# A hybrid decoder layer on one core: all tiles that TensorE reads at equal addresses modulo 256 bytes, V and index weights in three loads

## The chip, the cores and the metric

The kernel runs on one core of one Trainium2 chip. The metric is the device time of one execution in microseconds; several executions are timed, and their median is given.

## The reference

One decoder layer for 512 tokens of width 1,024, in float32. The input is normalised and multiplied by one wide matrix, whose columns feed two branches: a recurrent one (a short causal convolution, two gates, a scan over the tokens) and an attention one with 8 heads, in which index queries and keys choose 256 keys for each token. The branches are gated and added, then come an output projection, a gated channel mixer of width 3,072 with a convolution of length 3, and a gated embedding of the layer.

```
xn = _rmsnorm(x, mix_norm[l])
h = xn @ w_in[l]
lru_x, lru_gate, q, k, v, qi, ki, wi, gate_a, gate_b = _split_cols(h)
ya = (_rg_lru(...) * jax.nn.gelu(lru_gate)) @ w_lru_br[l]
yb = _dsa_attention(qh, kh, vh, qih, ki, wih, rel_bias) @ w_attn_br[l]
x = x + (jax.nn.sigmoid(gate_a) * ya + jax.nn.sigmoid(gate_b) * yb) @ w_out[l]
up = _rmsnorm(x, ffn_norm[l]) @ w_up[l]
x = x + (jax.nn.gelu(g_ffn) * up[..., D_FF:]) @ w_down[l]
x = x + jax.nn.sigmoid(_rmsnorm(x, ple_norm[l]) @ w_ple_gate[l]) * (p[l] @ w_ple_proj[l])
```

## The kernel before, in words

Features lie on the 128 partitions, the 512 tokens along them. Each float32 value is carried as two parts of the type float32r, a high one rounded to what one pass of TensorE takes and the low rest. A product is then three matmuls (`three`, lines 92 to 95): high weights with high data, high weights with low data, low weights with high data. Each names the weights (loaded into the array, 128 columns) and the moving data (mostly 512 columns).

The weights come as 155 slots of 128 partitions by 1,024 columns in `wall`, that is eight tiles of 128 x 128, and two wider ones of 1,056 columns for V and the index weights in `vwi` (eight k-tiles of 264 columns, four to a slot). For each slot three things happen. `load` (line 80) issues a DMA on SP's queue into one of two `raw` buffers. `split` (line 85) rounds it on ScalarE into a `whi` buffer (line 89) and subtracts on VectorE into a `wlo` buffer (line 90); there are four of each. Then a step function, `mm` for most (line 97), makes 24 matmuls on it, k-tile by k-tile, into a PSUM tile `acc`. All buffers are `WCOL` = 1,056 columns wide.

The order of the steps is a list written by hand (`add`, lines 589 to 717): projection, V and index weights (`vwi_step`, line 175), index keys, index queries, the recurrent branch with the attention's queries and keys between, gates, branch projection, attention, output projection, channel mixer, embedding gate. The loop at the end (lines 787 to 801) splits two slots ahead of the step and loads two ahead of the split. Work of the helpers, such as the choice of the keys and the recurrence, is put between the steps by budgets. The first two slots, and the norm of the input, are ordered by hand in lines 756 to 782: there the split of slot 3 (line 780) stands on ScalarE behind `norm_apply`.

`vwi_step` has the weights as moving data (264 columns) and `XN` in the array; four PSUM tiles stay open over both slots. `rel_bias` and the step `ki_step` follow.

The moving data of the steps: `XN` (normalised input; later merged branches, later the first 8 tiles of the mixer's hidden layer), `Y` (recurrent branch), `QO` (attention output), `XG` (input of mixer and of the last gate), `H` (the other hidden tiles). Index scores and attention also use `KK`, `QO`, `V`, `E`, `PT` and `dg`.

Tiles are placed per pool, one behind another in the order in which they are made. The base pool holds `XN` (32,768 bytes a partition), `F` (16,384), `vc` (744), `ident` and `ones` (512 each), `epsc` (8), `rstd` (2,048), then the `raw`, `whi` and `wlo` rings and `tmp`. Behind it comes the pool `mid` (`V`, `KK`, `QO`, `mask`, then `wi` of 128 bytes, `sp` of 192, `qs` of 128, and two each of `m8` with 32 and `sm` with 64), and behind that in turn the pools `start`, `lru` (with `Y` first) and `att` (`gb`, bias tiles, `E`, `dg`, `PT`). The mixer's pool (`H`, then `XG`, then `gp`) takes the place of `mid`.

```
for i in range(2, n):
    while ns <= min(i + 2, n - 1):
        split(ns)
        ns += 1
        while nl < min(ns + 2, n):
            load(nl)
            nl += 1
```

Of the kernel before, what the change touches and what calls it, by code (L numbers as in the profile page):

```python
# [10 lines left out]
F32 = mybir.dt.float32  # L11
# [5 lines left out]
T = 512  # L17
# [6 lines left out]
SENT = -3e38  # L24
ACAUSAL = -2e38
DROP = -1e30
WCOL = 1056

# columns of the packed per-partition vectors
V_MIX, V_FFN, V_PLE = 0, 8, 16  # L30
V_CW, V_CB, V_BA, V_BX, V_LAM = 24, 56, 64, 72, 80
V_QN, V_KN = 88, 89
V_FW, V_FB = 90, 162
V_N = 186

# rows of the packed weights
(S_PROJ, S_KI, S_QI, S_X, S_G, S_LG, S_A, S_BR, S_K, S_Q, S_B, S_AT, S_OUT, S_UP, S_DN, S_PG, S_END) = (
    0, 2, 3, 7, 15, 23, 25, 33, 41, 43, 51, 59, 67, 75, 123, 147, 155)

# [5 lines left out]
def layer(ctx: ExitStack, tc: tile.TileContext, xT, pT, wall, vwi, vec, relb, onehot, out):  # L45
    nc = tc.nc

    base = ctx.enter_context(tc.tile_pool(name="base", bufs=1))
# [4 lines left out]

    XN = base.tile([128, KT, 2, T], F32R, name="XN")
    F = base.tile([128, KT, T], F32, name="F")
    vc = base.tile([128, V_N], F32, name="vc")
    ident = base.tile([128, 128], F32, name="ident")
    ones_r = base.tile([128, 128], F32R, name="ones")
    ones = ones_r.bitcast(F32)
    epsc = base.tile([128, 2], F32, name="epsc")  # L60
    rstd = base.tile([128, T], F32, name="rstd")

    def tmp():
# [8 lines left out]
    def col(c):  # L72
        return vc[:, c:c + 1]

    # ------------------------------------------------------------------ weights
    RAW, HI, LO = {}, {}, {}
    LAST = [None]
    order = []

    def load(i):  # L80
        src, n = order[i][0]
        RAW[i] = base.tile([128, WCOL], F32, name="raw", bufs=NRAW)
        nc.sync.dma_start(RAW[i][:, :n], src)

    def split(i):
        n = order[i][0][1]
        HI[i] = base.tile([128, WCOL], F32R, name="whi", bufs=NSPL)
        LO[i] = base.tile([128, WCOL], F32R, name="wlo", bufs=NSPL)
        nc.scalar.copy(HI[i][:, :n], RAW[i][:, :n])  # L89
# [5 lines left out]
        nc.tensor.matmul(o, ll, rh, start=False, stop=stop)  # L95

    def mm(i, a, rhs, extras=(), first=True, last=True):
        """The products of one slot; extras are (k, function), called after the k-th tile."""
        ex = sorted(extras, key=lambda e: e[0])
        for k in range(KT):  # L100
            s = slice(k * 128, (k + 1) * 128)
            r = rhs(k)
            three(a, HI[i][:, s], LO[i][:, s], r[:, 0], r[:, 1], first and k == 0, last and k == KT - 1)
            while ex and ex[0][0] <= k:
                ex.pop(0)[1]()

    def pair(dst, src, g=None, lo=None):
        """dst[:, 0] + dst[:, 1] = src * g, the first rounded to what one pass carries."""
        if g is None:
            nc.scalar.copy(dst[:, 0], src)  # L110
            nc.vector.tensor_sub(dst[:, 1], src, dst[:, 0].bitcast(F32))
        else:
            nc.scalar.activation(dst[:, 0], src, AF.Copy, scale=g)
            nc.vector.scalar_tensor_tensor(dst[:, 1], src, g, dst[:, 0].bitcast(F32),
                                           op0=OP.mult, op1=OP.subtract)

    # ------------------------------------------------------------------ queues of background work
    urgent, patient, later = [], [], []
    credit = [0.0]

# [17 lines left out]
        for f, a in d:  # L138
            f(*a)

    # ------------------------------------------------------------------ phase pools
    mid = ExitStack()
    pm = mid.enter_context(tc.tile_pool(name="mid", bufs=1))
    V = pm.tile([128, NB, 2, 256], F32R, name="V")
    KK = pm.tile([128, 2, 2, T], F32R, name="KK")
    QO = pm.tile([128, HEADS, 2, T], F32R, name="QO")
    mask = pm.tile([128, 1280], F32, name="mask")
    wi = pm.tile([128, NB, 8], F32, name="wi")
    sp = pm.tile([128, 6, 8], F32, name="sp")
    qs = pm.tile([128, HEADS, NB], F32, name="qs")  # L150
    proj_d = dram.tile([128, KT, T], F32, name="proj_d")
    bv_d = dram.tile([HEADS, 640], F32, name="bv_d")
    bias_d = dram.tile([HEADS, 128, 640], F32, name="bias_d")
# [2 lines left out]
    att = ExitStack()  # L156
    P = {}

    # ------------------------------------------------------------------ step functions
    def xn(k):  # L160
        return XN[:, k]

    # index keys: KK[:, 0, 0] has the high part twice, KK[:, 0, 1] and KK[:, 1, 0] the low part in one half;
    # index queries: QO[:, m, z] has head 2m+z, the high part in half z, the low part in the other
    def ki_step(i):
        a = acc_tile()
        mm(i, a, xn)
# [4 lines left out]

    VP = []

    def vwi_step(i, half):
        if half == 0:
            VP.extend(aux_tile() for tb in range(NB))
        for kk in range(4):
            k = half * 4 + kk
            w = slice(kk * 264, kk * 264 + 264)  # L180
            for tb in range(NB):
                a = VP[tb][:, :264]
                s = slice(tb * 128, tb * 128 + 128)
                nc.tensor.matmul(a, XN[:, k, 0, s], HI[i][:, w], start=k == 0, stop=False)
                nc.tensor.matmul(a, XN[:, k, 0, s], LO[i][:, w], start=False, stop=False)
                nc.tensor.matmul(a, XN[:, k, 1, s], HI[i][:, w], start=False, stop=k == KT - 1)
        if half == 1:
            for tb in range(NB):
                a = VP[tb]
                nc.scalar.copy(V[:, tb, 0], a[:, :256])  # L190
                nc.vector.tensor_sub(V[:, tb, 1], a[:, :256], V[:, tb, 0].bitcast(F32))
                nc.vector.tensor_scalar_mul(wi[:, tb], a[:, 256:264], 8.0 ** -0.5)
# [34 lines left out]
        nc.vector.max(m8, sc)  # L227
        nc.vector.match_replace(sc, in_to_replace=m8, in_values=sc, imm_value=SENT)

    # recurrent branch  # L230
    def ua(m):
        return QO[:, m] if m in (4, 5, 6, 7) else P["Y"][:, m + 4]

# [64 lines left out]
        mm(i, a, lambda k: P["Y"][:, k])  # L298
        nc.vector.tensor_mul(F[:, m], F[:, m], a)

    # attention
    def k_step(i, n):
        a = acc_tile()
        mm(i, a, xn, held())
# [106 lines left out]
        nc.vector.tensor_add(t, t, F[:, m])  # L411
        defer(pair, XN[:, m], t)

    # sum of squares over the features, spread to every partition
    def square_in(m):
        if m == 0:
            nc.scalar.activation(rstd, F[:, 0], AF.Square)
# [5 lines left out]
            pair(XN[:, 0], rstd)  # L423

    def spread_sum(s, w):
        """The sum of the pair w over the partitions, on every partition."""
        nc.tensor.matmul(s, ones_r, w[:, 0], start=True, stop=False)
        nc.tensor.matmul(s, ones_r, w[:, 1], start=False, stop=True)

# [16 lines left out]
        defer(pair, P["XG"][:, m], F[:, m], col(V_FFN + m))  # L446
        defer(square_in, m)

    # channel mixer
    def hp(f):  # L450
        return XN[:, f] if f < 8 else P["H"][:, f - 8]

# [50 lines left out]
            nc.vector.tensor_add(t, t, F[:, m, c])  # L503
            nc.sync.dma_start(out[:, m, c], t)

    # ------------------------------------------------------------------ start
    pr = ExitStack()
    pp = pr.enter_context(tc.tile_pool(name="start", bufs=1))
    praw = pp.tile([128, 2, T], F32, name="praw")
# [48 lines left out]
        nc.scalar.dma_start(bv_d, bv)  # L558

    def softplus():  # L560
        """sp[:, 0] = 8 * softplus(-lambda), log1p by its odd series; sp[:, 1] = -sp[:, 0]."""
        rel_bias()
        lam = vc[:, V_LAM:V_LAM + 8]
        az, w, s, s2, acc = (sp[:, z] for z in (2, 3, 4, 5, 0))
        with tc.issue_after(P["last"].ins):
            nc.vector.scalar_tensor_tensor(az, lam, -1.0, lam, op0=OP.mult, op1=OP.max)
        nc.scalar.activation(w, az, AF.Exp, scale=-1.0)
        nc.vector.tensor_scalar_add(s, w, 2.0)
        nc.vector.reciprocal(s, s)
        nc.vector.tensor_mul(s, s, w)  # L570
        nc.vector.tensor_mul(s2, s, s)
        nc.vector.tensor_scalar(acc, s2, 1.0 / 17, 1.0 / 15, op0=OP.mult, op1=OP.add)
        for d in (13, 11, 9, 7, 5, 3, 1):
            nc.vector.tensor_mul(acc, acc, s2)
            nc.vector.tensor_scalar_add(acc, acc, 1.0 / d)
        nc.vector.tensor_mul(acc, acc, s)
        nc.vector.tensor_scalar(az, lam, -1.0, 0.0, op0=OP.mult, op1=OP.max)
        nc.vector.scalar_tensor_tensor(acc, acc, 2.0, az, op0=OP.mult, op1=OP.add)
        nc.vector.tensor_scalar_mul(sp[:, 1], acc, -8.0)
        nc.vector.tensor_scalar_mul(acc, acc, 8.0)  # L580
# [4 lines left out]
        if z == 3:  # L585
            pr.close()

    # ------------------------------------------------------------------ order of the steps
    def add(slot, fn, budget=0.0, before=None):
        src = slot if isinstance(slot, tuple) else (wall[slot], D)  # L590
        order.append((src, fn, budget, before))
# [13 lines left out]
    def open_ffn():  # L605
        att.close()
        mid.close()
        P["pool"] = ctx.enter_context(tc.tile_pool(name="ffn", bufs=1))
        P["H"] = P["pool"].tile([128, FT - 8, 2, T], F32R, name="H")
        P["XG"] = P["pool"].tile([128, KT, 2, T], F32R, name="XG")  # L610
        P["gp"] = [P["pool"].tile([128, T + 2], F32, name="gp%d" % z) for z in range(2)]
        for z in range(2):
            nc.gpsimd.memset(P["gp"][z][:, :2], 0.0)
        for m in range(2):
            load_x(m)
# [21 lines left out]
        add(S_Q + h, lambda i: q_step(i, h, pre, ex + held()), budget, before)  # L637

    def held():
        """What the steps before left for the tensor engine, to go in the middle of this one."""  # L640
        e = [(4, f) for f in P["held"]]
        P["held"] = []
        return e
# [2 lines left out]

    for z in range(2):
        add(S_PROJ + z, None)
    for z in range(2):
        add((vwi[:, z * WCOL:(z + 1) * WCOL], WCOL), lambda i, z=z: vwi_step(i, z), 0.0, None)  # L650
    def qi_before(m):
        if m == 0:
            softplus()
# [62 lines left out]
    for m in range(8):  # L716
        add(S_PG + m, lambda i, m=m: pg_step(i, m, [(7, stats)] if m == 0 else []), 0.0, lambda m=m: load_proj(m))

    # ------------------------------------------------------------------ run
    def proj_tile(i, m, a):  # L720
        c = m % 4
        for k in range(2):
# [11 lines left out]
    half = [slice(0, D // 2), slice(D // 2, D)]  # L734
    src, _ = order[0][0]
# [53 lines left out]
    for i in range(2, n):  # L789
# [7 lines left out]
        _, fn, budget, before = order[i]  # L797
# [68 lines left out]
```

## Time and profile before

| | us |
|---|---|
| runs | 962.04, 962.09, 963.38 |
| median | 962.09 |
| span of the profiled execution | 961.6 |
| TensorE busy in it | 948.0 |
| VectorE, ScalarE, GpSimd busy | 574.8, 434.7, 40.8 |

The span is the time from the first to the last instruction of the execution that the profiler recorded; no other time of that execution is given. Matmuls overlap: one of 512 columns is recorded with 0.39 us from start to end, while the next starts after less than 0.24. So TensorE's rate is read from starts, and the busy share tells only where it does not stop. PE stands for TensorE's matmuls, PEld for its weight loads, ACT for ScalarE, DVE for VectorE, POOL for GpSimd, SP for the engine whose queue issues the DMAs.

### The profile page before, as it was taken

The page shows a single profiled execution, that of the slowest core. Times are in us where ns is not written, and L with a number is a line of the kernel's source. Part 1 is how long each engine was busy: PE and PEld are TensorE (multiplying, and loading weights), DVE is VectorE, ACT ScalarE, POOL GpSimd, SP SyncE. Part 2 cuts the span into 40 slices and gives each one's busy share as a digit, 9 for nine tenths or more (in the row PEclk, how much of TensorE's full clock was granted, in tenths as well). Part 3 has the DMA queues.
Part 4 walks back from the last instruction along what each step waited for, and adds up shares of the span by engine and source line. Part 5 has one row for each costly group of instructions (what it writes and reads, how often), then busy time and mean ns, then how long its engine had stood idle before and what let it go on. Part 6 is the DMA issues. An engine that isn't in the chain of part 4 may idle for free.

```text
span 961.6 us, 11249 instructions
## 1 busy us (share of the span) xinstructions
PE 948.0 (99%) x4332; PEld 779.5 (81%) x4332; DVE 574.8 (60%) x915; ACT 434.7 (45%) x623; POOL 40.8 (4%) x44
## 2 busy tenths in 40 slices
PE   7999999999999999999999999999999999999997
PEld 5888788788888888888888888888888888888886
DVE  5769698689973757735556555554555533332373
ACT  6546776995212557742344333333333422222341
POOL 2000000000000000000000111111111100000000
PEclk9999999999999999999999999999999999999999
DMA  8561123114232311123442223223223223223242
GB/s 282 166 198 57 64 88 115 61 66 147 94 110 91 118 45 55 45 88 95 146 131 92 106 88 98 100 87 109 89 88 110 88 90 107 88 92 106 99 142 88
DMA packets 31172, 99.30 MB, mean 103 GB/s; under 512 B 3464, under 2 KB 3976, under 8 KB 31120
## 3 DMA queue, kind: packets, MB, share of 16 engines
q1 hardware_dynamic: 31104, 98.58, 31.1%
q8 instruction: 34, 0.56, 0.3%
q14 instruction: 18, 0.15, 0.0%
q10 hardware_dynamic: 16, 0.02, 0.0%
HBM read 94.37 MB, written 6.84 MB: 105 GB/s over the span
## 4 chain that ended last, share of the span: by engine, by line
PE 93%; DVE 3%; ACT 2%; DMA 1%; issue 0%; SPq 0%; DVEq 0%
PE acc L93 28%; PE acc L94 28%; PE acc L95 28%; PE aux L385 2%; PE aux L93 1%; PE aux L95 1%; PE aux L94 1%; PE aux L332 1%; DMA F<-in_xT 1%; DVE rstd L421 1%; DVE tmp L543 0%; ACT ri L264 0%; DVE XN L549 0%; PE aux L209 0%; PE aux L208 0%; DVE F L281 0%
## 5 line engine op out<-in xcount | busy, mean ns | idle before, releaser
L89 ACT CAST whi<-raw 128x1024 fp32r<-128x1024 f32 x156 | 163.7, 1050 | 371.0 <-PE acc L94 299.8
L90 DVE TENSOR_TENSOR wlo<-raw,whi 128x1024 fp32r<-128x1024 f32 x156 | 190.7, 1222 | 98.5 <-ACT whi L89 94.8
L93 PE MATMUL acc<-XN,whi 128*128 128x512 f32 x504 | 200.1, 397 | 0.1
L94 PE MATMUL acc<-XN,whi 128*128 128x512 f32 x504 | 199.5, 396 | 0.0
L95 PE MATMUL acc<-XN,wlo 128*128 128x512 f32 x504 | 199.3, 395 | 0.0
L93 PE MATMUL acc<-XG,whi 128*128 128x512 f32 (+1 forms) x456 | 177.1, 388 | 0.0
L95 PE MATMUL acc<-XG,wlo 128*128 128x512 f32 (+1 forms) x456 | 177.0, 388 | 0.0
L94 PE MATMUL acc<-XG,whi 128*128 128x512 f32 (+1 forms) x456 | 176.9, 388 | 0.0
L95 PEld LDWEIGHTS acc<-XN,wlo 128*128 128x128 f32 x504 | 94.7, 188 | 22.7
L93 PEld LDWEIGHTS acc<-XN,whi 128*128 128x128 f32 x504 | 94.7, 188 | 22.1 <-ACT whi L89 0.6
L94 PEld LDWEIGHTS acc<-XN,whi 128*128 128x128 f32 x504 | 94.8, 188 | 21.3
L95 PEld LDWEIGHTS acc<-XG,wlo 128*128 128x128 f32 x456 | 85.8, 188 | 18.5
L94 PEld LDWEIGHTS acc<-XG,whi 128*128 128x128 f32 x456 | 85.8, 188 | 18.4
L93 PEld LDWEIGHTS acc<-XG,whi 128*128 128x128 f32 x456 | 85.8, 188 | 18.3
L459 DVE TENSOR_TENSOR gp<-acc,rstd 128x512 f32<-128x512 f32 x24 | 16.6, 692 | 62.1 <-PE acc L95 62.0
L93 PE MATMUL acc<-H,whi 128*128 128x512 f32 x128 | 50.2, 392 | 0.0
L95 PE MATMUL acc<-H,wlo 128*128 128x512 f32 x128 | 50.2, 392 | 0.0
L94 PE MATMUL acc<-H,whi 128*128 128x512 f32 x128 | 50.2, 392 | 0.0
L472 DVE TENSOR_TENSOR tmp<-tmp,acc 128x512 f32<-128x512 f32 x24 | 16.5, 687 | 47.6 <-POOL tmp L465 47.6
L465 POOL TENSOR_TENSOR tmp<-tmp,rstd 128x512 f32<-128x512 f32 x24 | 31.0, 1290 | 278.0 <-ACT tmp L464 278.0
L93 PE MATMUL acc<-QO,whi 128*128 128x512 f32 x76 | 31.3, 411 | 5.3 <-ACT whi L759 5.3
L464 ACT ACTIVATE tmp<-tmp 128x512 f32<-128x512 f32 x24 | 15.2, 632 | 47.0 <-DVE tmp L463 47.0
(218 smaller groups left out, 1232.1 us busy)
## 6 DMA issues: line engine op xcount, KB each, us to landing
raw<-in_wall SPq DMA_DIRECT2D x154, 512.0 KB, 3.3
bias_d<-bv_d SPq DMA_DIRECT2D x8, 320.0 KB, 5.3
F<-in_xT SPq DMA_DIRECT2D x8, 256.0 KB, 6.0
proj_d<-pst SPq DMA_DIRECT2D x4, 512.0 KB, 3.8
bias<-bias_d SPq DMA_DIRECT2D x8, 256.0 KB, 2.7
tmp<-in_xT SPq DMA_DIRECT2D x8, 256.0 KB, 3.5
tmp<-proj_d SPq DMA_DIRECT2D x8, 256.0 KB, 3.4
out_dram<-tmp SPq DMA_DIRECT2D x7, 256.0 KB, 2.6
```

What stands on the lines that cost most here:

```text
L89: nc.scalar.copy(HI[i][:, :n], RAW[i][:, :n])
L90: LAST[0] = nc.vector.tensor_sub(LO[i][:, :n], RAW[i][:, :n], HI[i][:, :n].bitcast(F32))
L93: nc.tensor.matmul(o, lh, rh, start=start, stop=False)
L94: nc.tensor.matmul(o, lh, rl, start=False, stop=False)
L95: nc.tensor.matmul(o, ll, rh, start=False, stop=stop)
L332: nc.tensor.matmul(s[:, 2 * b:2 * b + 2], q2[:, b * 128:(b + 1) * 128], ones[:, :2], start=True, stop=True)
L385: nc.tensor.matmul(a[:, c:c + 128], E[h][:, SEG[b] + 128 * j:SEG[b] + 128 * j + 128], dg[:, b], start=True, stop=True)
L421: nc.vector.tensor_add(rstd, rstd, t)
L459: nc.vector.tensor_mul(gp[:, 2:], a, rstd)
L464: nc.scalar.activation(t, t, AF.Gelu_apprx_tanh)
L465: nc.gpsimd.tensor_mul(t, t, rstd)
L472: nc.vector.tensor_mul(t, GL[f], a)
```

## The change

`WCOL` becomes 1,024, so that each `raw`, `whi` and `wlo` buffer has 4,096 bytes a partition. `vc` and `epsc` become two views of one tile of 768 bytes. An unused tile of 128 bytes is added to the pool `mid`. The two `gp` tiles get 576 columns, of which 514 are used. The V and index weights are loaded in three slots of 3, 3 and 2 k-tiles. The rest of the diff removes comments.

```diff
-WCOL = 1056
...
+WCOL = 1024
+
+VW = 264
+VPARTS = [(0, 3), (3, 6), (6, 8)]
...
-    vc = base.tile([128, V_N], F32, name="vc")
+
+
+    vce = base.tile([128, 192], F32, name="vc")
+    vc, epsc = vce[:, :V_N], vce[:, V_N:V_N + 2]
...
-    epsc = base.tile([128, 2], F32, name="epsc")
...
+    pm.tile([128, 32], F32, name="rest")
...
-    def vwi_step(i, half):
-        if half == 0:
+    def vwi_step(i, part):
+        if part == 0:
             VP.extend(aux_tile() for tb in range(NB))
-        for kk in range(4):
-            k = half * 4 + kk
-            w = slice(kk * 264, kk * 264 + 264)
+        for k in range(*VPARTS[part]):
+            w = slice((k - VPARTS[part][0]) * VW, (k - VPARTS[part][0] + 1) * VW)
             for tb in range(NB):
-                a = VP[tb][:, :264]
+                a = VP[tb][:, :VW]
...
-        if half == 1:
+        if part == 2:
...
-        P["gp"] = [P["pool"].tile([128, T + 2], F32, name="gp%d" % z) for z in range(2)]
+        P["gp"] = [P["pool"].tile([128, 576], F32, name="gp%d" % z)[:, :T + 2] for z in range(2)]
...
-    for z in range(2):
-        add((vwi[:, z * WCOL:(z + 1) * WCOL], WCOL), lambda i, z=z: vwi_step(i, z), 0.0, None)
+    for z, (k0, k1) in enumerate(VPARTS):
+        add((vwi[:, k0 * VW:k1 * VW], (k1 - k0) * VW), lambda i, z=z: vwi_step(i, z), 0.0, None)
```

## Rows read from the trace of the kernel before

**Rows 1.** The page: span, and busy time of each engine.
```profile
span 961.6 us, 11249 instructions
...
PE 948.0 (99%) x4332; PEld 779.5 (81%) x4332; DVE 574.8 (60%) x915; ACT 434.7 (45%) x623; POOL 40.8 (4%) x44
```

**Rows 2.** Who waited for whom, TensorE: us in total, times, longest.
```profile
PE acc L93 <- ACT whi L759: 5.3, 1, 5.3
```

**Rows 3.** TensorE's groups by shape: count | busy us, mean ns | idle before.
```profile
L93 PE MATMUL acc<-XN,whi 128*128 128x512 f32 x504 | 200.1, 397 | 0.1
...
L93 PE MATMUL acc<-XG,whi 128*128 128x512 f32 x440 | 172.6, 392 | 0.0
...
L93 PE MATMUL acc<-H,whi 128*128 128x512 f32 x128 | 50.2, 392 | 0.0
...
L93 PE MATMUL acc<-QO,whi 128*128 128x512 f32 x76 | 31.3, 411 | 5.3 <-ACT whi L759 5.3
...
L93 PE MATMUL acc<-Y,whi 128*128 128x512 f32 x64 | 25.1, 392 | 0.0
```

**Rows 4.** Timeline of TensorE, channel mixer: start us, latency us, engine, line, tiles.
```profile
547.12 0.39 PE L93 MATMUL acc<-XG,whi 128*128 128x512 f32 x1
...
552.56 0.39 PE L93 MATMUL acc<-XG,whi 128*128 128x512 f32 x1
...
558.01 0.40 PE L93 MATMUL acc<-XG,whi 128*128 128x512 f32 x1
...
569.17 0.39 PE L93 MATMUL acc<-XG,whi 128*128 128x512 f32 x1
```

**Rows 5.** Busy time by stretch: steps on XN; on Y slow; on Y fast.
```profile
222.00:266.80 44.80, 44.80 (x193) 36.06 (x192) 43.62 (x97) 15.57 (x21) 0.00 (x0) 1.00 0.36 119
294.30:305.50 11.20, 11.20 (x50) 9.05 (x49) 3.82 (x4) 2.14 (x3) 0.00 (x0) 1.00 0.28 94
283.40:294.30 10.90, 10.90 (x49) 9.02 (x49) 3.82 (x4) 2.10 (x2) 0.00 (x0) 1.00 0.34 115
```

**Rows 6.** Timeline, V and index weights: start us, us, engine, line, tiles [idle before].
```profile
30.14 0.28 PE L184 MATMUL aux<-whi,XN 128*128 128x264 f32 x1
...
31.16 1.06 ACT L89 CAST whi<-raw 128x1056 fp32r<-128x1056 f32 x1
...
31.46 0.28 PE L186 MATMUL aux<-whi,XN 128*128 128x264 f32 x1
...
32.27 0.75 PE L184 MATMUL aux<-whi,XN 128*128 128x264 f32 x4 [0.53 <-ACT whi L89]
...
33.01 1.24 DVE L90 TENSOR_TENSOR wlo<-raw,whi 128x1056 fp32r<-128x1056 f32 x1
...
34.28 0.33 SPq L83 DMA_DIRECT2D raw<-in_wall  x1
...
38.74 1.05 ACT L89 CAST whi<-raw 128x1024 fp32r<-128x1024 f32 x1 [1.20 <-DMA raw<-in_wall]
...
40.06 0.28 PE L186 MATMUL aux<-whi,XN 128*128 128x264 f32 x1
...
41.93 1.05 ACT L89 CAST whi<-raw 128x1024 fp32r<-128x1024 f32 x1 [1.60 <-DMA raw<-in_wall]
...
44.10 1.21 DVE L90 TENSOR_TENSOR wlo<-raw,whi 128x1024 fp32r<-128x1024 f32 x1
```

**Rows 7.** Busy time by stretch, and timeline: weights split just in time.
```profile
112.00:120.00 8.00, 8.00 (x36) 6.42 (x35) 2.77 (x4) 7.97 (x13) 0.00 (x0) 1.00 0.00 0
...
126.27 1.20 DVE L90 TENSOR_TENSOR wlo<-raw,whi 128x1024 fp32r<-128x1024 f32 x1
...
127.85 0.39 PE L95 MATMUL acc<-XN,wlo 128*128 128x512 f32 x1
...
214.91 1.20 DVE L90 TENSOR_TENSOR wlo<-raw,whi 128x1024 fp32r<-128x1024 f32 x1
...
216.89 0.39 PE L95 MATMUL acc<-XN,wlo 128*128 128x512 f32 x1
```

## The prediction

> **What bounds the kernel now.** I read the page first. TensorE is busy 948.0 of 961.6 us, the other engines 60% or less [rows 1]; and the longest of TensorE's waits, in the view of who waited for whom, is 5.3 us for the very first weights; the three others there are shorter by far [rows 2]. So the time is the number of matmuls times the distance from one start to the next (the pitch), and a change of addresses has to show there or nowhere. The groups of TensorE by shape give the number: 504 x 3 = 1,512 matmuls of 512 columns move XN, 440 x 3 = 1,320 XG, 384 H, 228 QO and 192 Y, 3,636 in all [rows 3].
>
> Then the pitch. In the channel mixer, where all steps have the same shape, 48 matmuls (two steps) from 547.12 to 558.01 us take 10.89 us, the next 48 to 569.17 take 11.16: 226.9 and 232.5 ns; the first step alone, to 552.56, has 226.7 [rows 4]. The pattern two fast steps, two slow steps goes on through the whole mixer. The stretches say the same: eight steps on XN in 44.80 us are 192 matmuls of 233.3 ns, though TensorE never stops in them; a pair on Y takes 11.20 us when slow and 10.90 when fast [rows 5] (each count holds one or two matmuls that reach in). The granted clock is 1.00 in all of them, 2.4 GHz.
>
> What differs between two neighbouring pairs is the slot of the weight ring alone. The trace has no addresses; they follow from the widths of the tiles, which lie one behind another in units of 32 bytes. Counted modulo 256 from XN: F, vc (744, padded to 768), ident and ones end on 0; epsc's 8 bytes push all that follows to 32. A weight slot of 1,056 x 4 = 4,224 bytes is 16 x 256 + 128, so raw, whi and wlo slots lie at 32 and 160 in turn. V, KK, QO, and later H and XG, are at 32; the small tiles behind mask sum to 640 bytes, so Y, E and PT are at 160. The ring takes its slots so that two steps at 32 follow two at 160. With this: XG, H, QO (32) and Y (160) match the weights in half of their steps, and those are the fast ones; the slots that are fast under XG are slow under Y. XN (0) never matches and is always slow. Equal residue 226.8, 128 apart 232.5, 32 or 160 apart 233.3 ns.
>
> **The change part by part.** *Matching.* epsc moves into vc's padding (768 bytes for both), a weight slot becomes 4,096 bytes, and 128 bytes of filler bring the small tiles to 768: XN, weights, V, KK, QO, Y, E, PT, H and XG all come to residue 0. XN: 1,512 x (233.3 - 226.7) = 10.0 us. The other 2,124: half of them, 1,062 x (232.5 - 226.7) = 6.2, and 0.2 for the first matmuls of matched steps, which still come late (226.9 against 226.7). Sum 16.4. Bounds: 15.6 with the smallest differences that these rows give (5.5 and 6.5 ns), 17.2 if every mismatched matmul loses the 6.6 of XN. The matmuls of 264 columns and fewer I cost at nothing: a V slice starts 1,056 bytes after the last, so they stay unequal.
>
> *gp and the removed comments.* gp gets wider, but TensorE doesn't read it and nothing it reads lies behind it: nothing.
>
> *V and index weights in three slots.* Each part needs its own load, cast on ScalarE and subtraction on VectorE, and the raw ring has two slots. Now the first half, four k-tiles, keeps TensorE going until 31.46 us; the second waits 0.53 us for its cast, which starts at 31.16 behind the norm's last copies, and ends at 32.22 [rows 6]. With three k-tiles the first part is over where k-tile 3 begins now, 12 matmuls earlier, at 30.14: from there to 31.46 are eleven starts of 0.12 us (0.28 is a latency), so 1.44 us of work now lie behind the wait. The cast is of 792 columns instead of 1,056, a quarter shorter, 0.25 us. So +1.2. Until the second half's low part is there (subtraction from 33.01 to 34.25) TensorE fills the time with two matmuls of the index-key step among others; that step's weights now come one slot later, so these fillers go: +0.3 with what the cast's end leaves open. Its load takes the turn in SP's queue that the first query load has now (34.28 issued, cast at 38.74 after 1.20 us for the DMA, over at 39.79, the low part some 1.2 us later); the last V matmul, at 40.06 now, would start at about 41.5, so it is just in time. One more load is issued by SP (0.33 us), one more small cast and subtraction; the V matmuls cover these. Sum +1.5. Ends: -0.3 if only the shorter cast counts and TensorE finds other work, +3.8 if the key weights come with the second load in that row (cast at 41.93, low part from 44.10 to 45.31, 3.8 us after 41.5). I take 1.5, as the first load's turn is nearest.
>
> *What is late next.* A faster TensorE eats slack that ScalarE and VectorE keep before it. Between 112 and 120 us ScalarE is busy 7.97 of 8 us; at 126.27 a subtraction of 1.20 us ends 0.38 us before the matmul at 127.85 that reads it; the one at 214.91 ends at 216.11, its reader is at 216.89, 0.78 us [rows 7]. Over the 23 us in which ScalarE has no idle time (104 to 127) matching gives TensorE some 0.6 us, of which 0.38 are free; before the second point ScalarE and VectorE are full for about 60 us, worth 1.7, of which 0.78 are free, but part of that work starts when TensorE lets it. I take 1.0 us given back; ends 0 and 4.5 (the 5.7 that 200 us on XN give, less both slacks). From 230 us on weights are split many microseconds ahead.
>
> Sum: -16.4 + 1.5 + 1.0 = -13.9 us on the profiled 961.6. The page gives no time beyond the span; the median of the runs is 962.1, 0.5 above, so **948.2**. The bounds add to 962.1 - 17.2 - 0.3 = 944.6 and 962.1 - 15.6 + 3.8 + 4.5 = 954.8.
>
> **The rivals.**
> 1. *The helpers bind* up to 280 us: the whole 4.5 is given back and the weights of the key step come late by about 1.5 more. 948.2 + 3.5 + 1.5 = 953.2. For it: the two slacks. Against: neither slack has become a wait of TensorE today.
> 2. *Addresses don't matter*, and the two speeds have another cause. Then only the V slots count: 962.1 + 1.5 = 963.6. For it: no step on XN is fast, whatever the slot. Against: one shape, one clock, one program line, and the speed turns with the slot [rows 4]. The Trainium skill states this rule (TensorE: Matmul & The Clock Gate, "What happens when you issue a matmul"): the array has two independent read ports, and loading the next weights takes nothing from the running matmul. By it the change gains nothing. The trace speaks against it.
> 3. *Slower: XN's own residue is the slow one.* No row has TensorE reading XN and weights at the same residue. If moving data at XN's place is slow by itself, the change carries all tiles there: the matched half, 1,062, loses 6.6 ns each (7.0 us), the 128-apart half 0.8 (0.8 us), the V slots 1.5: 962.1 + 9.3 = 971.4. It decides if steps on XN stay at 5.600 us. For it: all 1,512 are slow. Against: 32 and 160 are alike for Y and XG, and there the difference alone decides.
> 4. *The change doesn't do what it says*: the later pools land 128 off, so that XN gains 10.0 and the other half loses 6.2: 962.1 - 10.0 + 6.2 + 1.5 = 959.8, a difference of 0.24%, at the limit of what can be told.
>
> **How the numbers follow.** Forecast 0.78 (its own range 944.5 to 951.5), rival 1 0.10, rival 2 0.04, rival 3 0.05, rival 4 0.03. The range 944.5 to 954.0 takes in the forecast and most of rival 1. About 0.2% (1.9 us) can be told from no change. Faster: 0.78 + 0.10 = 0.88. Within: rival 4 and most of rival 2, 0.07. Slower: rival 3, 0.05.
>
> **What would show it.** Right: every step of 24 takes 5.44 us, those on XN too; the spread between neighbouring pairs is gone; TensorE's busy time falls to about 932; a longer idle time of TensorE, near 2 us, before the second V part around 30 us; new short waits of the key step's weights or at 127 and 217 us. Wrong: XN at 5.600 (rival 3), pairs that still alternate (rival 4 or 2), VectorE or ScalarE named in TensorE's waits with more than 3 us (rival 1).

## The result and the profile after

The change makes the kernel faster: 948.57 us (947.85 to 949.27, four runs) against 962.74 (962.04 to 963.86, four runs), a ratio of 0.9851 with a 95% interval of 0.9837 to 0.9865, or 14.2 us. The forecast was 948.2 in a range of 944.5 to 954.0. The profiled execution is the fastest of the four: 947.85 us, with a span of 946.1.

The page of the changed kernel, span and busy time of the engines [rows 1]:

```profile
span 946.1 us, 11256 instructions
...
PE 931.9 (99%) x4332; PEld 776.9 (82%) x4332; DVE 575.1 (61%) x916; ACT 435.4 (46%) x624; POOL 40.5 (4%) x44
```

TensorE makes the same 4,332 matmuls in 16.1 us less; no other engine has less to do (VectorE and ScalarE have one instruction more, for the third slot).

The timeline of TensorE in the channel mixer, the first matmul of steps on four different slots of the weight ring [rows 4]:

```profile
543.38 0.39 PE L98 MATMUL acc<-XG,whi 128*128 128x512 f32 x1
548.82 0.39 PE L98 MATMUL acc<-XG,whi 128*128 128x512 f32 x1
554.26 0.39 PE L98 MATMUL acc<-XG,whi 128*128 128x512 f32 x1
...
565.14 0.39 PE L98 MATMUL acc<-XG,whi 128*128 128x512 f32 x1
```

From 543.38 to 554.26 two steps take 10.88 us, the next two, to 565.14, again 10.88: 226.7 ns a matmul on every slot, where before it was 226.9 and 232.5 in turn. Over the whole trace the undisturbed steps on XN, XG, H, Y and QO all take 5.440 us.

The stretches that answer to [rows 5], steps on XN and two pairs on Y; the columns are PE, PEld, DVE, ACT, POOL busy, the granted clock, DMA share and GB/s:

```profile
213.00:257.00 44.00, 44.00 (x194) 36.16 (x193) 42.94 (x87) 17.25 (x23) 0.00 (x0) 1.00 0.36 120
280.00:291.00 11.00, 11.00 (x50) 9.13 (x49) 4.29 (x5) 2.11 (x2) 0.00 (x0) 1.00 0.40 139
291.00:302.00 11.00, 11.00 (x50) 9.10 (x49) 3.96 (x5) 2.10 (x2) 0.00 (x0) 1.00 0.29 95
```

On XN 194 matmuls now need 44.00 us, before it was 193 in 44.80; the two stretches on Y have the same count in the same time. The clock is 1.00 as before, so the gain is not one of the clock.

What TensorE waits for, by line: us in total, times, longest [rows 2]:

```profile
PE aux L189 <- ACT whi L94: 1.2, 1, 1.2
...
PE aux L561 <- ACT bv L562: 0.6, 1, 0.6
PE aux L337 <- ACT tmp L332: 0.6, 1, 0.6
```

These three belong to the change: 1.2 us before the second V part, 0.6 before the last two bias matmuls (line 561), and 0.6 at line 337, a statistic of the queries. The timeline of the first two:

```profile
27.79 0.28 PE L191 MATMUL aux<-whi,XN 128*128 128x264 f32 x1
...
28.94 0.83 ACT L94 CAST whi<-raw 128x792 fp32r<-128x792 f32 x1
...
29.83 0.75 PE L189 MATMUL aux<-whi,XN 128*128 128x264 f32 x4 [1.21 <-ACT whi L94]
...
30.79 0.97 DVE L95 TENSOR_TENSOR wlo<-raw,whi 128x792 fp32r<-128x792 f32 x1
...
31.16 0.81 PE L561 MATMUL aux<-oh,rb 128*128 128x320 f32 x2 [0.58 <-ACT bv L562]
...
31.81 0.39 PE L190 MATMUL aux<-wlo,XN 128*128 128x264 f32 x1
...
36.97 1.05 ACT L94 CAST whi<-raw 128x1024 fp32r<-128x1024 f32 x1 [2.44 <-DMA raw<-in_wall]
...
38.05 1.23 DVE L95 TENSOR_TENSOR wlo<-raw,whi 128x1024 fp32r<-128x1024 f32 x1 [0.84 <-ACT whi L94]
...
38.92 0.39 PE L99 MATMUL acc<-XN,whi 128*128 128x512 f32 x1
39.33 0.51 PE L100 MATMUL acc<-XN,wlo 128*128 128x512 f32 x1
39.67 0.40 PE L98 MATMUL acc<-XN,whi 128*128 128x512 f32 x1
```

The first part, now three k-tiles, ends with the matmul at 27.79. The second part's cast is only 0.83 us long, but still stands behind the norm's last copies on ScalarE and starts at 28.94; TensorE waits until 29.83. Its low half is there at 31.76. In between TensorE has four matmuls with the high half and the bias matmuls, and stands still again. Further on, the key step's weights are cast at 36.97, and their low half is there at 39.28; the step's first matmul with it starts at 39.33. That is 0.41 us behind its neighbour, and the next follows after 0.34, some 0.3 us lost in both.

Where the 15.5 us between the two spans (961.6 and 946.1) lie: the V matmul that waits for the first normalised tile starts at 22.79 instead of 24.99, 2.2 us earlier; from there the V stage takes 1.4 us longer, so that the first query step starts at 44.49 instead of 45.31; from there to the end it is 901.6 us instead of 916.3, 14.7 less. The 2.2 us are no gain of the change. The start in the kernel before, with the columns of the stretch as above, and behind it the same two matmul groups in the changed kernel:

```profile
15.03 1.05 PE L520 MATMUL aux<-ones,rstd 128*128 128x2 f32 x8 [1.58 <-DVE rstd L421]
...
18.25 1.91 PE L529 MATMUL aux<-dgn,ones 128*128 128x128 f32 x8
...
16.80:20.30 3.50, 3.50 (x13) 3.12 (x13) 1.96 (x5) 2.11 (x5) 0.00 (x0) 0.51 0.75 236
...
14.41 1.05 PE L525 MATMUL aux<-ones,rstd 128*128 128x2 f32 x8 [0.78 <-DVE rstd L426]
...
16.92 1.05 PE L534 MATMUL aux<-dgn,ones 128*128 128x128 f32 x8
```

The statistic of the input came 0.6 us sooner (14.41). The other 1.6 us lie between there and the end of the second group (15.03 to 20.16 before, 14.41 to 17.97 now) and go with TensorE's clock. In the kernel before, TensorE had stood 1.58 us for the statistic, and from about 16.8 to 20.3 us its granted clock was at the lower level, 1.2 GHz (0.51 in the stretch); the eight matmuls that spread the norm's factor took 1.91 us instead of 1.05. In this execution of the changed kernel it had stood 0.78 us, and the granted clock is 1.00, that is 2.4 GHz, over the same stretch. So what the two traces give the change is the rest, 14.7 - 1.4 = 13.3 us.

### The profile page after: what moved, and what is told of

Read it like the earlier page. It is cut to its first block, busy times and chain, and to the rows that moved or that the text cites. A ratio compares the mean times of both kernels' runs of the same rounds, so it can differ in the third digit from the quotient of the medians.

```text
span 946.1 us, 11256 instructions
## 1 busy us (share of the span) xinstructions
PE 931.9 (99%) x4332; PEld 776.9 (82%) x4332; DVE 575.1 (61%) x916; ACT 435.4 (46%) x624; POOL 40.5 (4%) x44
## 4 chain that ended last, share of the span: by engine, by line
PE 93%; DVE 3%; ACT 3%; DMA 1%; issue 0%; SPq 0%; DVEq 0%
PE acc L98 28%; PE acc L100 28%; PE acc L99 28%; PE aux L390 2%; PE aux L98 1%; PE aux L100 1%; PE aux L99 1%; PE aux L337 1%; DMA F<-in_xT 1%; DVE rstd L426 1%; ACT ri L269 1%; DVE tmp L548 1%; DVE XN L554 0%; PE aux L214 0%; PE aux L213 0%
## 5 line engine op out<-in xcount | busy, mean ns | idle before, releaser
L94 ACT CAST whi<-raw 128x1024 fp32r<-128x1024 f32 (+1 forms) x157 | 164.2, 1046 | 360.0 <-PE acc L99 281.6
L95 DVE TENSOR_TENSOR wlo<-raw,whi 128x1024 fp32r<-128x1024 f32 (+1 forms) x157 | 191.0, 1217 | 96.3 <-ACT whi L94 95.1
L98 PE MATMUL acc<-XN,whi 128*128 128x512 f32 x504 | 197.4, 392 | 0.0
L100 PE MATMUL acc<-XN,wlo 128*128 128x512 f32 x504 | 196.9, 391 | 0.0
L99 PE MATMUL acc<-XN,whi 128*128 128x512 f32 x504 | 196.9, 391 | 0.0
L477 DVE TENSOR_TENSOR tmp<-tmp,acc 128x512 f32<-128x512 f32 x24 | 16.5, 688 | 47.3 <-POOL tmp L470 47.3
L468 DVE SCALAR_TENSOR_TENSOR tmp<-gp,vc,tmp 128x512 f32<-128x512 f32 x48 | 36.0, 749 | 0.8
```

The lines of the kernel that those rows point to most:

```text
L95: LAST[0] = nc.vector.tensor_sub(LO[i][:, :n], RAW[i][:, :n], HI[i][:, :n].bitcast(F32))
L98: nc.tensor.matmul(o, lh, rh, start=start, stop=False)
L99: nc.tensor.matmul(o, lh, rl, start=False, stop=False)
L468: nc.vector.scalar_tensor_tensor(t, gp[:, j:j + T], col(V_FW + 24 * j + f), t, op0=OP.mult, op1=OP.add)
L477: nc.vector.tensor_mul(t, GL[f], a)
```

## The experiments

Kernels that ran once are judged by their traces rather than by their times. Times of steps are of 24 matmuls, from the first start to the first start of the next step.

**V in three slots alone.** The kernel before, with widths as they were:

```diff
+VW = 264
+VPARTS = [(0, 3), (3, 6), (6, 8)]
...
-    for z in range(2):
-        add((vwi[:, z * WCOL:(z + 1) * WCOL], WCOL), lambda i, z=z: vwi_step(i, z), 0.0, None)
+    for z, (k0, k1) in enumerate(VPARTS):
+        add((vwi[:, k0 * VW:k1 * VW], (k1 - k0) * VW), lambda i, z=z: vwi_step(i, z), 0.0, None)
```

> The kernel before, with the V and index weights in three slots and nothing else: all tiles stay where they were. If the pitch goes with the difference of the addresses, only the V stage moves: the steps keep 5.60 us on XN and alternate between 5.44 and 5.58 in the mixer, and the time is 1.5 us longer than before (0.16%; between -0.3 and +3.8). If the three slots had a part in the gain, it comes out faster than before.

963.52 us (962.14 to 965.30, 11 runs) against 961.89 for the kernel before on that chip (15 runs): ratio 1.0018, interval 1.0009 to 1.0027, a loss of 1.6 us. TensorE's new wait is the same as in the changed kernel:

```profile
PE aux L186 <- ACT whi L92: 1.2, 1, 1.2
```

The steps keep both paces: 5.600 us on XN, 5.444 to 5.446 and 5.572 to 5.585 in turn on XG. So this part of the change costs time by itself, and all of the gain comes from the widths.

But the 1.6 us are not the waiting alone. In the profiled execution (965.00 us) TensorE's granted clock fell to 1.2 GHz twice ahead of the query steps, the second time within the V stage, behind stops of 1.21 and 0.57 us:

```profile
33.26:36.67 3.41, 3.41 (x15) 3.01 (x15) 1.60 (x4) 1.86 (x3) 0.00 (x0) 0.50 0.99 286
```

The times go with the mean granted clock: one run at 0.999 took 962.14 us, six at 0.997 or 0.998 took 963.12 to 963.67, four at 0.996 took 964.82 to 965.30. The kernel before has seven runs at 0.999 or 1.000, with 961.39 to 961.98, and none under 0.997. So part of the loss is time at the lower clock; how large a part, one run at 0.999 can't tell. The trace of the changed kernel has the same stops (1.21 and 0.58) and no fall behind them; why the clock falls in one execution and not in another is open.

**Equal addresses without three slots.** From the changed kernel: `raw` goes back to 1,056 columns, and `whi` and `wlo` become 1,088 wide, 4,352 bytes, which is 17 x 256; V comes in two halves again.

```diff
-WCOL = 1024
+WCOL = 1056
+SCOL = 1088
...
-VPARTS = [(0, 3), (3, 6), (6, 8)]
+VPARTS = [(0, 4), (4, 8)]
...
-        HI[i] = base.tile([128, WCOL], F32R, name="whi", bufs=NSPL)
+        HI[i] = base.tile([128, SCOL], F32R, name="whi", bufs=NSPL)
```

> The changed kernel with V and index weights in two slots again: the split weight buffers are 1,088 columns wide (4,352 bytes, 17 times 256), so that all tiles that TensorE reads still have one residue. If matching is the whole gain and the three slots a cost, every step of 24 takes 5.44 us and the time is about 1.5 us under the changed kernel, some 947; no wait of 1.2 us before the second V part. If a width of 1,024 itself matters, the steps are slower than 5.44 us.

948.12 us (946.79 to 948.92, four runs), ratio 0.9856 (0.9841 to 0.9871): by the times alone it can't be told from the changed kernel. The traces can, both at a mean granted clock of 1.000 (946.79 and 947.85 us): all undisturbed steps take 5.44 us here too, the V stage, counted from the matmul that waits for the first normalised tile, is 1.6 us shorter, and the last matmul ends 1.4 us earlier. The wait before V's second half is short:

```profile
PE aux L190 <- ACT whi L95: 0.5, 1, 0.5
```

Two things follow. The price of the three slots is about 1.4 us here too. And slots 17 x 256 bytes apart are all fast, as slots 16 x 256 apart are in the changed kernel; those 16.5 x 256 apart were fast and slow in turn. Among multiples of 256 odd and even do not differ.

**Eight distances in two kernels.** From the changed kernel, `whi` and `wlo` slots of 1,032 columns, 4,128 bytes, so that each slot lies 32 bytes further modulo 256 than the last; two unused tiles bring `whi` and `wlo` of the same slot to the same distance from the moving tiles. In the first kernel the four distances are 0, 32, 64 and 96, in the second 128, 160, 192 and 224 (an unused tile stands ahead of the ring). The moving tiles stay where they were.

```diff
+SCOL = 1032
...
+    base.tile([128, 32], F32, name="fill0")
+    HI[0] = base.tile([128, SCOL], F32R, name="whi", bufs=NSPL)
+    base.tile([128, 32], F32, name="fill1")
+    LO[0] = base.tile([128, SCOL], F32R, name="wlo", bufs=NSPL)
```

(The second kernel; the first has no `fill0`, and a `fill2` behind `wlo`.)

> The changed kernel with the four slots of the split weights at distances 0, 32, 64 and 96 bytes from all moving tiles (modulo 256); the tiles read as moving data stay where they are. If the difference modulo 256 decides: 5.44 us per step for the slot at 0 and 5.58 to 5.60 for 32, with 64 and 96 like 32; three quarters of 3,636 matmuls lose about 6.2 ns, so the time is some 17 us over the changed kernel, about 965. If only the place within 64 bytes counts, the slot at 64 is as fast as that at 0, and the time is about 957. If addresses don't matter, all four are alike.

> The same with the four slots at distances 128, 160, 192 and 224. If the difference modulo 256 decides: no step is at 5.44 us; 128 gives 5.58 (before: 232.5 ns), 160 gives 5.60 (233.3), 192 and 224 near these; the time is some 22 us over the changed kernel, about 970, above the kernel before. If the distance counts modulo 64 or 128 alone, the slots at 128 and 192, or at 128, are as fast as 5.44.

968.95 and 969.71 us, one run each, with the kernel before at 961.89. Their mean granted clocks are 0.996 and 0.995, so that the times hold more than the steps. The timelines in the mixer, first matmuls of successive steps, and within the step at 549.87 two matmuls more. The trace has no addresses; worked out from the program, the steps meet the slots of the first kernel in the order 0, 96, 32, 64. The list begins at 96:

```profile
533.07 0.39 PE L99 MATMUL acc<-XG,whi 128*128 128x512 f32 x1
...
538.69 0.39 PE L99 MATMUL acc<-XG,whi 128*128 128x512 f32 x1
...
544.27 0.40 PE L99 MATMUL acc<-XG,whi 128*128 128x512 f32 x1
...
549.87 0.39 PE L99 MATMUL acc<-XG,whi 128*128 128x512 f32 x1
...
551.26 0.39 PE L99 MATMUL acc<-XG,whi 128*128 128x512 f32 x1
...
552.62 0.39 PE L99 MATMUL acc<-XG,whi 128*128 128x512 f32 x1
...
555.34 0.39 PE L99 MATMUL acc<-XG,whi 128*128 128x512 f32 x1
```

In the second kernel, a step at 192 from 544.26 and the next, at 128, from 549.76:

```profile
544.26 0.39 PE L99 MATMUL acc<-XG,whi 128*128 128x512 f32 x1
...
549.76 0.39 PE L99 MATMUL acc<-XG,whi 128*128 128x512 f32 x1
...
555.35 0.40 PE L99 MATMUL acc<-XG,whi 128*128 128x512 f32 x1
```

In the first list distance 0 takes 5.47 us (549.87 to 555.34), 96 takes 5.62, 32 takes 5.58 and 64 takes 5.60. In the second 192 takes 5.50 and 128 takes 5.59. Read with more digits over all steps on XG and H: 5.471 us at 0 (where the steps before and behind are unequal), 5.589 at 32, 5.598 at 64, 5.615 at 96, 5.593 at 128, 5.603 at 160, 5.499 to 5.513 at 192 and 5.604 at 224. XN, XG, H, QO and Y agree at each distance to within 0.03 us. Moving the weights alone brings the slow pace back under every moving tile. That alone could be the place of the weights; but in the kernel before, the same weight slots were fast under Y (at 160) and slow under XG (at 32), and the other way round. So it is the difference of the two addresses, and not the place of XN or of the weights. 192 had not been expected: it loses less than half of what the others lose.

The step at 0 is not at the matched pace throughout. Behind the step at 64 its first six matmuls take 1.39 us (549.87 to 551.26), the next six 1.36, which is 226.7 ns each: the slower pace lasts into the step, though own and next weights are at 0 from its first matmul on.

**Which matmul of the three is slow.** From the changed kernel, two unused tiles, one before and one behind `wlo`: the low weights lie 128 away from the moving tiles, the high ones at 0.

```diff
+SCOL = 1024
...
+    HI[0] = base.tile([128, SCOL], F32R, name="whi", bufs=NSPL)
+    base.tile([128, 32], F32, name="fill1")
+    LO[0] = base.tile([128, SCOL], F32R, name="wlo", bufs=NSPL)
+    base.tile([128, 32], F32, name="fill2")
```

> The changed kernel with all low weights 128 bytes away (modulo 256), high weights and moving tiles as in it. Of a k-tile's three matmuls the first runs while high weights are loaded, the second while low ones are, the third while the next high ones are. If a running matmul is slowed by the weights that are loaded meanwhile, one in three is slow: the step takes 24 x 226.7 + 8 x 6.0 = 5.49 us, and the matmul with high weights and low data (the second) has the long distance to the next start. If its own weights count, the third has it. If every unequal tile slows the whole stream, the step takes 5.58. Time some 7 us over the changed kernel, 955, or 22 over it.

964.75 us, one run; every step takes 5.546 us. The timeline in the mixer, four matmuls in a row (line 99 is high weights with high data, 100 high with low, 101 low with high):

```profile
558.64 0.40 PE L101 MATMUL acc<-XG,wlo 128*128 128x512 f32 x1
558.88 0.39 PE L99 MATMUL acc<-XG,whi 128*128 128x512 f32 x1
559.10 0.40 PE L100 MATMUL acc<-XG,whi 128*128 128x512 f32 x1
559.34 0.40 PE L101 MATMUL acc<-XG,wlo 128*128 128x512 f32 x1
```

The distances to the next start are 0.24, 0.22 and 0.24 us; averaged over some 1,200 matmuls of each line they are 234.0 ns for line 101, 227.0 for 99 and 232.4 for 100. Line 99 has its own weights at 0, and those loaded meanwhile (the next matmul's) are at 0 too: it alone is fast. Line 100 has its own at 0 but the next at 128, line 101 the other way round. So at a distance of 128 both count: the weights that are in the array and those that are loaded for the next matmul. Neither of the two simpler readings, own weights alone or next weights alone, gives two slow matmuls of three. A full rule this is not: the six slow matmuls at the head of the step at 0 (above) have both at 0.

**The early split.** Equal addresses with two V halves, as above, and in addition the split of the fourth slot (V's second half) no longer stands behind the norm: its cast comes after the third tile of the norm, its subtraction after the seventh.

```diff
-    def norm_apply(bc, between):
+    def norm_apply(bc, between, hi3, lo3):
...
             nc.scalar.activation(XN[:, k, 0], t[k], AF.Copy, scale=col(V_MIX + k))
+            if k == 2:
+                hi3()
+            if k == 6:
+                lo3()
...
-        split(3)
```

> The matched kernel with V in two slots and the split of its second slot earlier in the order of ScalarE and VectorE: the cast behind the norm's third copy, in a gap where ScalarE waits for VectorE, the subtraction before the low part of k-tile 6. If the second V part waits for the split alone, its wait of 0.5 us and the fillers after it go: 0.9 us under the matched kernel with two slots, some 947. If the subtraction holds up the norm's last tiles instead, the same or up to 1 us slower.

947.53 us (946.63 to 947.93, five runs), ratio 0.9846 (0.9832 to 0.9859). Against the version with two halves and the old order the intervals overlap, and at the same clock the times are the same: the two runs at a mean granted clock of 0.999 took 946.63 and 946.79 us, the other version's run at 1.000 took 946.79. In the traces the V stage is 0.7 us shorter, but 0.4 of that is lost again behind it, 0.25 at the first matmul of the query steps, and the last matmul ends 0.3 us earlier (939.75 against 940.02). The expected 0.9 did not come: the wait of 0.5 us before V's second half is still there, now for its low part.

**Fine distances.** From the changed kernel, slots of 1,088 columns of which the weights use 1,024, beginning at column 1, 2, 4 or 6 (4, 8, 16 and 24 bytes above the moving tiles), and in a second kernel at column 63, 62, 60 or 58 (4, 8, 16 and 24 bytes below, that is 252, 248, 240 and 232).

```diff
+SCOL = 1088
+OFF = [1, 2, 4, 6]
...
-        HI[i] = base.tile([128, WCOL], F32R, name="whi", bufs=NSPL)
+        HI[i] = base.tile([128, SCOL], F32R, name="whi", bufs=NSPL)[:, OFF[i % 4]:OFF[i % 4] + WCOL]
```

> The changed kernel with the four slots of the split weights at distances 4, 8, 16 and 24 bytes from all moving tiles. If only what 32-byte units differ in counts, all four have 5.44 us per step. If equality must be exact, all four have 5.58 to 5.60. If it goes over gradually, the steps grow from 5.44 with the distance.

> The same with distances of -4, -8, -16 and -24 bytes (252, 248, 240, 232). If the units of 32 bytes count, all four are like 224, at 5.60. If it goes over gradually, they lie between 5.44 and 5.60. If some distance other than 0 is better than 0, a step comes out under 5.44 here or with the positive distances.

965.52 and 959.00 us, one run each, with the kernel before at 962.54. Above: 5.57 to 5.58 us at 4 bytes, 5.54 at 8, 5.60 at 16, 5.52 or 5.545 at 24. Below: 5.447 at 4 bytes (with a few steps of 5.59), 5.596 at 8, 5.482 at 16, 5.543 at 24. Two of these in the timeline of the second kernel, a step at 248 from 526.89 and one at 252 from 543.51:

```profile
526.89 0.39 PE L100 MATMUL acc<-XG,whi 128*128 128x512 f32 x1
...
532.48 0.39 PE L100 MATMUL acc<-XG,whi 128*128 128x512 f32 x1
...
543.51 0.39 PE L100 MATMUL acc<-XG,whi 128*128 128x512 f32 x1
...
548.96 0.40 PE L100 MATMUL acc<-XG,whi 128*128 128x512 f32 x1
```

5.59 and 5.45 us. Neither a grid of 32 bytes nor a loss that grows with the distance fits: 4 bytes above cost 5.7 ns a matmul, 4 bytes below nearly nothing, 8 below 6.5. No distance is better than 0.

**The best version beside the changed kernel.** The changed kernel unaltered, and the early split once more, on one chip.

> The changed kernel once more, unaltered, as the yardstick for the run beside it on the same chip. Theory (V and index weights in three slots cost 1.4 us at the start, as the trace of the changed kernel shows): about 948.6, the median of its first timing. Rival (the three slots cost nothing once the addresses are equal): the same as the run beside it within 0.5 us.

> Equal addresses with V in two slots, and the fourth split drawn into the norm, beside the changed kernel on the same chip, with more runs. Theory: 1.3 to 1.7 us less than the changed kernel (1.4 from the V slots, up to 0.3 from the earlier split), near 947.1. Rival: no difference over 0.5 us; the 1 us between the medians of the earlier timings was scatter.

948.91 us (948.06 to 951.09) and 946.91 (946.74 to 947.00), four runs each; the ratios to the kernel before are 0.9872 (0.9856 to 0.9889) and 0.9844 (0.9829 to 0.9858). The runs of the two don't overlap, and the medians are 2.0 us apart, 0.3 more than the theory gave at most. That surplus goes with the clock: the changed kernel's runs at a mean granted clock of 0.999 took 948.06 and 948.14 us, the two at 0.997 and 0.996 took 949.69 and 951.09, and the other kernel has no run under 0.999. Runs at 0.999 or more are 1.1 to 1.4 us apart, about the price of the three V slots alone; of a gain from the earlier split nothing is to be seen. TensorE's wait before the second V part of the changed kernel is as before:

```profile
PE aux L189 <- ACT whi L94: 1.2, 1, 1.2
```

The last operation of VectorE that the timeline shows starts 1.8 us earlier in the early split (941.23 against 943.03). Its own timeline shows what is left to wait for:

```profile
22.69 1.06 ACT L95 CAST whi<-raw 128x1056 fp32r<-128x1056 f32 x1
...
29.25 1.25 DVE L99 TENSOR_TENSOR wlo<-raw,whi 128x1056 fp32r<-128x1056 f32 x1
...
30.55 0.39 PE L198 MATMUL aux<-wlo,XN 128*128 128x264 f32 x1 [0.51 <-DVE wlo L99]
```

The second half's high part is there from 23.75 us on, long before TensorE comes to it; what is late is the low part, by half a microsecond.

## Why the prediction was right

**Matching, forecast -16.4.** Right in mechanism and nearly in size. The steps came out at 5.440 us for all tiles, as forecast. From the first query step to the start of the last matmul the time fell from 911.05 us to 896.65, by 14.4; the other 0.3 of the 14.7 lie behind the last matmul. With the 1.0 of new short stops of TensorE in that stretch (below) the pace of the matmuls gave 15.4. The steps ahead of it add about 0.3, worked out and not measured: the key step 24 x 6.6 ns, the projection's 36 matmuls half of 5.8 each. That is 15.7 of 16.4. TensorE's busy time, forecast at about 932, is 931.9, but that it agrees so well is luck: 1.8 of the 16.1 us by which it fell lie between the input's statistic and the V matmuls (9.66 us busy before, 7.90 after), where the kernel before ran at the lower clock.

**V in three slots, forecast +1.5.** In the traces 1.4 against the kernel before, and 1.4 at the last matmul against the version with two halves. The place is right too: 1.2 us before the second part. The key step's weights, which the forecast called just in time, came some 0.3 us late: the cast begins at 36.97, which is 39.2 when the 2.2 us by which the V matmuls began earlier are put back, where the forecast took 38.74 from the row. What the forecast did not have is the clock, which fell within the V stage in the trace with three slots and the old widths.

**The sum.** With what was measured it is -15.7 + 1.4 + 1.0 = -13.3 us, where the forecast had -13.9; the medians give -14.2 on one chip and -12.9 on another (961.79 and 948.91). The forecast took the profiled 961.6 for 0.5 us less than the median. In the runs on record the time lies 1.7 us or more above the span, so the profiled execution must have been the slowest of the three, 963.38 us, with the stretch at 1.2 GHz in it; as only the difference was carried over to the median, this did not enter the forecast.

**Helpers, forecast +1.0.** The size is right, the place only in part. Two points were named, the subtractions that end just ahead of their matmuls [rows 7]. The later one does appear, at 213: the pitch is 0.37 and 0.34 us for two matmuls instead of 0.23. The earlier one, expected at about 126, hardly shows; in its place a wait at 134 that was not named:

```profile
133.81 0.39 PE L100 MATMUL acc<-XN,wlo 128*128 128x512 f32 x1
134.75 0.94 PE L337 MATMUL aux<-ones,tmp 128*128 128x2 f32 x7 [0.55 <-ACT tmp L332]
...
212.97 0.39 PE L99 MATMUL acc<-XN,whi 128*128 128x512 f32 x1
213.34 0.50 PE L100 MATMUL acc<-XN,wlo 128*128 128x512 f32 x1
213.68 0.40 PE L98 MATMUL acc<-XN,whi 128*128 128x512 f32 x1
```

The statistic of the queries needs the square that ScalarE makes of `acc` behind VectorE's copy of it, and VectorE's scans of the recurrence stand ahead of that copy:

```profile
131.60 1.22 DVE L286 TENSOR_TENSOR_SCAN F<-ri,ri 128x512 f32<-128x512 f32 x1
...
133.32 0.75 DVE L119 SCALAR_TENSOR_TENSOR QO<-acc,vc,QO 128x512 fp32r<-128x512 f32 x1
```

The copy ends at 134.07, the square runs from 134.10 to 134.70. In the kernel before the same matmul came 0.52 us after its neighbour, now it is 0.94. The other stops are of 0.1 us each, at 107, 124 and 167. The step of the prediction that failed is the choice of the point: it looked for the least slack among the weights' splits, and did not follow the chains of the other helpers to TensorE.

**The rivals.** The helpers did not bind: no wait on ScalarE or VectorE behind the V stage is over 0.6 us. That addresses don't matter falls with the eight distances. The rule of the Trainium skill that stood beside this rival (TensorE: Matmul & The Clock Gate, "What happens when you issue a matmul"), that loading the next weights takes nothing from the running matmul, does not hold here for the distance between starts: in the kernel with the low weights 128 bytes off, at one clock and with the same high weights in the array, it was 227.0 ns when the weights loaded meanwhile lay at 0 and 232.4 when they lay at 128. XN's own place is not slow: at equal residue its steps take 5.440 us. And the later pools landed where the widths said: XG and H are as fast as XN.

What stays open is the mechanism. The runs show when a matmul is slow; they do not show why the loss is 7 ns at one distance and next to none at another, and no run here looked into what the weight load and the moving data share. Nor do they show why the clock fell in some executions only.

## What to carry to other kernels

When matmuls of one shape and one clock have two paces that turn with the slot of a ring, work out the addresses of both operands: here a slot that is a multiple of 256 bytes wide, and moving tiles at the same residue, were worth 1.6% of a kernel that TensorE bounds, at no cost in instructions. Pad the slot rather than cut the load to fit it: slots that are padded keep the loads as they are, and the three loads that the narrower slots asked for gave 1.4 us back. When two versions are a microsecond apart, compare runs of the same granted clock before you explain the difference. Before such a gain is added up, look where the helpers' chains reach TensorE, because a faster TensorE meets each of them earlier.

## What the runs showed of the hardware that was not expected

The loss is not a step function of the distance. Of sixteen distances modulo 256, only 0 gives 226.7 ns in all steps (of the changed kernel); 252 gives 226.9 in most steps, 240 gives 228.4, 192 between 229.1 and 229.7, 24, 8 and 232 between 230 and 231, and the other nine 232.2 to 234.0, all worked out as the step's time over 24. Small steps one way are not like small steps the other way (4 bytes above: 232.2 to 232.4; 4 below: 226.9). At a distance of 128 a matmul is slowed by the weights of its successor nearly as much as by its own (232.4 and 234.0 against 227.0); at 96 the successor's weights did less (228.5 ns over the 35 matmuls that end a step at 0 ahead of one at 96). And the slow pace outlasts the unequal weights: after a step at 64 the first six matmuls of the step at 0 took 1.39 us, the next six 1.36.

TensorE's clock fell in some executions of a kernel and not in others, at a cost of about a microsecond each time. Of the runs whose clock is on record, eight have a mean granted clock under 0.997, and all eight are of kernels with V in three slots, which stop TensorE for 1.2 and 0.6 us in the V stage; none is of a kernel with two.
